# Attention scores of a hybrid decoder: 288 contraction rows as three passes of 96, or as two passes of 128 and remainders of 32 rows taken two at a time

## The chip, the core and the metric

The program runs on one core of one Trainium2 chip. The metric is the device time of one execution in microseconds (us). Before the change it is 3236.64 us, the median of three runs (3236.11 to 3240.59). Engine names are those of the profile: PE is the matmul array, PEld its weight loads, DVE, ACT and POOL the vector, scalar and general engines, SP the engine that only issues transfers. "SPq" and "POOLq" are the queues of transfers that these two issue.

## What is computed

A Mamba-2 layer, then a layer of multi-head latent attention with 16 heads over 2048 positions, then a final norm; the batch is 1, and everything is float32. The part that the change touches is the causal attention (cut to what matters):

```
Q_BLOCK = 128;  QK_NOPE, QK_ROPE, V_HEAD = 64, 32, 64
for i in range(2048 // Q_BLOCK):                      # queries q0 .. q0 + 127
    kv_len = (i + 1) * Q_BLOCK                        # keys 0 .. kv_len - 1
    s = q_nope @ k_nope.T + q_rope @ k_rope.T         # a contraction over 64 + 32 = 96
    p = softmax(where(causal, scale * s, -inf))
    out = p @ v                                       # then gate and output projection
```

`k_nope` and `q_nope` differ from head to head; `k_rope` (32 rows) is one for all 16 heads.

## The kernel before

**Numbers.** Every matmul operand is split into a high part and a low part (`hi`, `lo`), and a product is taken as hi by hi, hi by lo and lo by hi. The helper `mm3` (L83 to L87) issues these three as matmuls on one PSUM bank: L85, L86, L87. The same three lines serve all projections of the program, so the profile lists them under many operand names. For the scores their operands are `K` and `xT`, where a tile named `xT` of this stage is a block of queries (the pool that gave the normalised inputs is used again).

**Tiles of the attention.** The scores of a head need a tile `K` of [96, 2, 2048] (64 rows of `k_nope`, 32 rows of `k_rope`; the middle index is hi or lo) and for each of four blocks of 512 queries a tile `Q` of [96, 2, 512]. `load_k` (L829) issues two transfers on POOL's queue (L834, L835), `load_q` (L842) three (L846 to L848). They are asked for one head ahead: `scores(h, qb)` asks at its start for the queries of (h + 1, qb), and at qb = 2 for the keys and values of head h + 1.

**Loops.** `scores(h, qb)` (L878) runs over j = 0..3, the four groups of 128 queries of a block. The keys up to the diagonal, qb*512 + (j + 1)*128 of them, are cut by `cuts` (L869) into chunks of 512, with a last one of 512, 384 or 256. Each chunk takes one PSUM bank `s` of [128, 512] under the name `mm`; there are four of these and four of the name `tr`. A chunk is three matmuls, on the last chunk of a j also a matmul that adds the causal mask (L904 or L906), and then DVE takes the maximum of each row (L907, into `mx`). After a j's last chunk DVE forms the negated maximum `nm` (L911), and `exp` (L917 to L919) has ACT write exp(s + nm) to a tile `Pr`; only then is the bank free. These exponentials are handed out one at a time, one ahead of each chunk of the next j (`late`, L895), so that chunk n of a j finds its bank freed by the exponential of the chunk four earlier.

A head has 40 such chunks: 1 in each j of block 0, 2 in each j of block 1, 3 in each j of block 2 and 4 in each j of block 3.

**The order on PE** is written by hand (`manual_schedule`). `scores` is a generator that yields after each chunk a string of credits from a table `CREDIT`. A "T" has PE transpose one block of 128 keys of an earlier query block (L934, four transposes into a `tr` bank), which ACT and DVE then turn into a pair of f16 tiles `PTs` (L116, L117). A "V" has PE multiply such a pair by the values (L944, L945, f16). For block 3 the strings of j = 3 are "TV", "V", "", "TVTVT". So between two chunks PE does up to some five other units, or none. T and V lag behind the scores by 20 chunks. The order on the other engines is chosen by a scheduler; their instructions start in that order. `finish` (L949) has ACT copy a finished output bank to `Os` (L951), which SP stores (L953) and POOL adds to (L957).

Of the kernel before, what the change touches and what calls it, by code (L numbers as in the profile page):

```python
# [9 lines left out]
F32 = mybir.dt.float32  # L10
F32R = mybir.dt.float32r
# [4 lines left out]
ALU = mybir.AluOpType  # L16
AX = mybir.AxisListType
# [3 lines left out]
P = 128  # L21
T = 2048
# [6 lines left out]
TB = 512  # L29
NB = T // TB  # L30
# [12 lines left out]
CREDIT = (  # L43
    (("VT",), ("TV",), ("VT",), ("TV",)),
    (("", "VTVT"), ("", "TTVV"), ("", "TTVV"), ("", "TTVV")),
    (("TT", "", "VVTV"), ("TV", "", "VTTV"), ("TV", "", "TTVV"), ("TTV", "", "TVV")),
    (("T", "", "", "VVTTVTV"), ("T", "V", "", "VTTVTV"), ("T", "V", "V", "TVTTV"), ("TV", "V", "", "TVTVT")),
)
# [20 lines left out]
class Net:  # L69
# [409 lines left out]
    def ssd(self, b, g):  # L479
# [21 lines left out]
        for c in range(4):  # L501
# [31 lines left out]
            with self.tc.high_priority(20):  # L533
                v.tensor_tensor(v8(Xd), v8(px), heads(dt), ALU.mult)  # L534
# [13 lines left out]
            if not first:  # L548
                pi = self.t(self.pp, "tr", [P, TB], bufs=4)
                self.mm3(pi, Ct[:, 0], Ct[:, 1], old[:, 0], old[:, 1], True, True)  # L550
                t = self.t(self.sp, "yt", [P, TB], bufs=2)
                v.tensor_tensor(v8(t), v8(pi), heads(ecum), ALU.mult)
                v.tensor_tensor(y, y, t, ALU.add)
            yield
            if not last:
                pst = self.t(self.pp, "tr", [P, TB], bufs=4)
                self.mm3(pst, Bt[:, 0], Bt[:, 1], Xp[:, 0], Xp[:, 1], True, True)
                if first:
                    st = self.state[g] = self.t(self.sp, f"st{g}", [P, TB], bufs=1)
                    v.tensor_copy(st, pst)  # L560
                else:
                    st = self.state[g]
                    v.tensor_tensor(v8(st), v8(st), heads(dec), ALU.mult)
                    v.tensor_tensor(st, st, pst, ALU.add)
                if c < 3:
                    old = halves(pair("Sp", TB, 1), st)
# [261 lines left out]

    def load_k(self, h, lo, hi):  # L829

        nc, ts = self.nc, slice(lo * TB, hi * TB)
        if lo == 0:
            self.keys[h] = self.t(self.hp, "K", [96, 2, T], F32R, bufs=2)
        nc.gpsimd.dma_start(self.keys[h][0:64, :, ts], self.kn_d[h * 64:(h + 1) * 64, :, ts])  # L834
        nc.gpsimd.dma_start(self.keys[h][64:96, :, ts], self.kr_d[:, :, ts])  # L835

    def load_v(self, h):

# [2 lines left out]

    def load_q(self, h, n):  # L842

        nc, ts = self.nc, slice(n * TB, (n + 1) * TB)
        Q = self.quer[h, n] = self.t(self.xq, "xT", [96, 2, TB], F32R, bufs=8)
        nc.gpsimd.dma_start(Q[0:64], self.qn_d[h * 64:(h + 1) * 64, :, ts])  # L846
        nc.gpsimd.dma_start(Q[64:80], self.q1_d[h * 16:(h + 1) * 16, :, ts])
        nc.gpsimd.dma_start(Q[80:96], self.q2_d[h * 16:(h + 1) * 16, :, ts])  # L848

    def load_wo(self, k):  # L850

# [12 lines left out]
    def heads(self, sp):  # L864
        nc, v = self.nc, self.nc.vector
        begun = []
        keys, vals, quer = self.keys, self.vals, self.quer

        def cuts(kv):  # L869

            out, at = [], 0
            while at < kv:
                w = min(TB, kv - at)
                if kv - at == TB + P:
                    w = 384
                out.append((at, max(w, 256)))
                at += w
            return out  # L878

        def scores(h, qb, st):  # L880

            if h + 1 < NH:
                if qb == 2:
                    self.load_k(h + 1, 0, NB)
                    self.load_v(h + 1)
                self.load_q(h + 1, qb)
            Q, K = quer.pop((h, qb)), keys[h]
            late = []
            for j in range(4):
                qs = slice(j * P, (j + 1) * P)  # L890
                parts = cuts(qb * TB + (j + 1) * P)
                nb = len(parts)
                mx = self.t(sp, "mx", [P, 4], bufs=4)
                banks = []
                for n, (c0, w) in enumerate(parts):  # L895
                    if late:
                        late.pop(0)()
                    begun.append(0)
                    s = self.t(self.pp, "tr" if len(begun) <= 18 and len(begun) % 2 == 1 else "mm", [P, TB], bufs=4)
                    ks = slice(c0, c0 + w)  # L900
                    self.mm3(s[:, :w], Q[:, 0, qs], Q[:, 1, qs], K[:, 0, ks], K[:, 1, ks], True, n < nb - 1)
                    if n == nb - 1:
                        if qb == j == 0:
                            nc.tensor.matmul(s[:, 0:w], self.idb, self.mk, start=False, stop=True)  # L904
                        else:
                            nc.tensor.matmul(s[:, w - P:w], self.idb, self.mk[:, 0:P], start=False, stop=True)  # L906
                    v.tensor_reduce(mx[:, n:n + 1], s[:, :w], AX.X, ALU.max)  # L907
                    banks.append((s, w))
                    yield CREDIT[qb][j][n]
                nm = self.t(sp, "nm", [P, 1], bufs=4)  # L910
                v.tensor_reduce(nm, mx[:, :nb], AX.X, ALU.max, negate=True)  # L911
                p = {}
                sm = self.t(sp, "sm", [P, 4], bufs=4)
                st["P"].append(p)

                def exp(n, j=j, nb=nb, parts=parts, banks=banks, nm=nm, p=p, sm=sm):
                    s, w = banks[n]  # L917
                    x = self.t(sp, "Pr", [P, TB], bufs=NP)
                    nc.scalar.activation(x[:, :w], s[:, :w], AF.Exp, bias=nm, accum_out=sm[:, n:n + 1])  # L919
                    for c in range(0, w, P):  # L920
                        p[(parts[n][0] + c) // P] = x[:, c:c + P]
                    if n == nb - 1:
                        v.tensor_reduce(sums[h][:, 4 * qb + j:4 * qb + j + 1], sm[:, :nb], AX.X, ALU.add)

                late += [lambda n=n, f=exp: f(n) for n in range(nb)]
            for f in late:
                f()
# [43 lines left out]
        def ahead():  # L971
            for n, (h, qb) in enumerate(jobs):
                if qb == 0:
                    sums[h] = self.t(sp, "sum", [P, 16], bufs=3)
                yield from scores(h, qb, states[n])
# [215 lines left out]
```

## Time and profile before

| | |
|---|---|
| median of three runs | 3236.64 us |
| the profiled execution, its span | 3237.6 us |
| attention stage, first score to last | about 2127 to 3050 us |
| PE busy over the whole span | 3132.7 us (97%) |
| DVE, ACT, POOL busy over the span | 80%, 63%, 20% |
| granted TensorE clock | 9 tenths or more in each of 40 slices |
| moved by the transfers | 419.04 MB, 129 GB/s on the mean |

The profiled execution is one run of its own; its span, 3237.6 us, is the one time known of it, and it is 1.0 us over the median. A row of groups in the profile reads: line, engine, operation, out<-in by the names of the program, tile of the array (rows*columns), shape, count, then busy us and mean ns of one, then the idle time of the engine ahead of these instructions and what ended it. Matmuls are pipelined: the next begins to stream while the one before still drains, so the duration of a matmul (0.39 us) is not what it costs; the distance of two starts is (0.23 us). A matmul that follows one of another kind is shown with a start that is too early and a duration that is too long by the same amount; the start of the next matmul on the same engine is right.

### The profile page before, as it was taken

How to read it: one execution, taken by the hardware profiler on the slowest of the kernel's cores; microseconds unless marked ns; L12 is line 12 of the kernel's file. 1: busy time of each engine (PE TensorE's matmuls, PEld its weight loads, DVE VectorE, ACT ScalarE, POOL GpSimd, SP SyncE). 2: the span in 40 equal slices, each digit the busy share in tenths (PEclk: the TensorE clock that was granted, in tenths of full speed). 3: DMA queues.
4: the chain of work that ended last, by engine and by line, in shares of the span. 5: the costliest groups of instructions: out<-in, count | busy, mean ns of one | idle time of the engine just before them, and what ended most of it. 6: DMA issues, size and time to landing. Idle time of an engine off the chain costs nothing.

```text
span 3237.6 us, 52523 instructions
## 1 busy us (share of the span) xinstructions
PE 3132.7 (97%) x17732; PEld 2510.0 (78%) x17732; DVE 2593.3 (80%) x5490; ACT 2053.9 (63%) x5117; POOL 646.5 (20%) x842
## 2 busy tenths in 40 slices
PE   8999999999999999998999999999999999999998
PEld 6778777787787777877788888777777777777787
DVE  6888888888889788898776765668888888888675
ACT  5666666656667656666555554467777878778522
POOL 1221122221212212222211211222212221222100
PEclk9999999999999999999999999999999999999999
DMA  5333334333433334333466666754443534444395
GB/s 174 108 94 98 119 123 130 100 94 120 147 99 105 92 125 140 108 95 118 127 232 209 234 209 203 243 135 80 84 86 78 100 74 89 79 88 115 81 276 167
DMA packets 210579, 419.04 MB, mean 129 GB/s; under 512 B 27106, under 2 KB 68834, under 8 KB 208868
## 3 DMA queue, kind: packets, MB, share of 16 engines
q1 hardware_dynamic: 168900, 291.39, 29.4%
q0 software_dynamic: 41408, 124.29, 15.9%
q8 instruction: 140, 2.29, 0.3%
q14 instruction: 131, 1.07, 0.1%
HBM read 321.33 MB, written 94.24 MB: 128 GB/s over the span
## 4 chain that ended last, share of the span: by engine, by line
PE 42%; DMA 3%; DVE 3%; ACT 3%; issue 1%; SPq 0%; POOL 0%; ACTq 0%; DVEq 0%
PE mm L85 7%; PE mm L87 6%; PE mm L86 6%; PE tr L934 6%; PE tr L944 3%; PE tr L945 3%; PE tr L86 3%; PE tr L87 3%; PE tr L85 3%; DMA os<-ri_d 1%; ACT Pr L919 1%; DVE PTs L117 1%; ACT PTs L116 1%; DMA os<-o_d 1%; PE mm L906 1%
## 5 line engine op out<-in xcount | busy, mean ns | idle before, releaser
L117 DVE SCALAR_TENSOR_TENSOR PTs<-tr,PTs 128x512 f16<-128x512 f32 (+3 forms) x640 | 374.7, 607 | 93.1 <-ACT PTs L116 86.9
L116 ACT ACTIVATE PTs<-tr 128x512 f16<-128x512 f32 (+3 forms) x640 | 328.4, 541 | 140.1 <-PE tr L934 139.3
L907 DVE TENSOR_REDUCE mx<-mm 128x1 f32<-128x512 f32 (+2 forms) x631 | 375.3, 607 | 45.3 <-PE mm L87 42.7
L919 ACT ACTIVATE Pr<-mm,nm 128x512 f32<-128x512 f32 (+2 forms) x631 | 395.5, 636 | 23.0 <-DVE nm L911 21.4
L109 DVE TENSOR_TENSOR wsp<-wraw,wsp 128x512 fp32r<-128x512 f32 (+1 forms) x452 | 301.7, 679 | 78.2 <-ACT wsp L108 77.4
L108 ACT ACTIVATE wsp<-wraw 128x512 fp32r<-128x512 f32 (+1 forms) x452 | 252.1, 573 | 171.9 <-DMA wraw<-in_ssm_w_in_dram 66.2
L85 PE MATMUL mm<-xT,wsp 128*128 128x512 f32 x800 | 322.0, 403 | 0.0
L934 PE MATMUL tr<-pack,Pr 128*128 128x128 f32 x2176 | 317.5, 273 | 1.5 <-ACT Os L951 1.4
L87 PE MATMUL mm<-xT,wsp 128*128 128x512 f32 x800 | 314.3, 393 | 0.0
L86 PE MATMUL mm<-xT,wsp 128*128 128x512 f32 x800 | 313.5, 392 | 0.0
L85 PE MATMUL mm<-K,xT 96*128 96x512 f32 (+2 forms) x639 | 286.6, 449 | 23.3 <-ACT Pr L919 21.9
L934 PEld LDWEIGHTS tr<-pack,Pr 128*128 128x128 f32 x2176 | 253.4, 141 | 49.8 <-ACT Os L951 2.2
L85 PE MATMUL mm<-wsp,xT 128*128 128x512 f32 (+1 forms) x640 | 243.0, 380 | 3.8 <-ACT craw L352 3.1
L87 PE MATMUL mm<-wsp,xT 128*128 128x512 f32 (+1 forms) x640 | 237.5, 372 | 0.0
L86 PE MATMUL mm<-wsp,xT 128*128 128x512 f32 (+1 forms) x640 | 237.5, 371 | 0.0
L87 PE MATMUL mm<-K,xT 96*128 96x512 f32 (+2 forms) x639 | 231.5, 362 | 0.0
L86 PE MATMUL mm<-K,xT 96*128 96x512 f32 (+2 forms) x639 | 231.0, 362 | 0.0
L358 DVE SCALAR_TENSOR_TENSOR cacc<-craw,pack,cacc 128x512 f32<-128x512 f32 x288 | 214.9, 766 | 16.0 <-ACT cacc L356 15.5
L944 PE MATMUL tr<-PTs,xT 128*128 128x512 f16 (+3 forms) x640 | 222.0, 348 | 0.1
L496 POOL TENSOR_TENSOR Xp<-Xw,Xp 128x512 fp32r<-128x512 f32 x64 | 83.4, 1303 | 691.5 <-ACT Xp L495 478.5
L945 PE MATMUL tr<-PTs,xT 128*128 128x512 f16 (+3 forms) x640 | 219.4, 347 | 0.0
L538 ACT ACTIVATE Xw<-tr,d_wend 128x64 f32<-128x64 f32 x512 | 183.4, 359 | 51.0 <-DVE Xd L534 51.0
(368 smaller groups left out, 8050.4 us busy)
## 6 DMA issues: line engine op xcount, KB each, us to landing
wraw<-in_ssm_w_in_dram SPq DMA_DIRECT2D x256, 256.0 KB, 2.7
big<-cumT SPq DMA_DIRECT2D x64, 512.0 KB, 4.4
wraw<-in_ssm_w_out_dram SPq DMA_DIRECT2D x128, 256.0 KB, 2.7
wraw<-in_ssm_w_in_dram SPq DMA_DIRECT2D x129, 128.0 KB, 2.3
xT<-qn_d POOLq DMA_DIRECT2D x64, 256.0 KB, 4.5
K<-kn_d POOLq DMA_DIRECT2D x15, 1024.0 KB, 9.4
wraw<-in_mla_w_uq_dram SPq DMA_DIRECT2D x36, 256.0 KB, 4.0
hx<-in_x_dram SPq DMA_DIRECT2D x16, 512.0 KB, 4.8
```

The costliest lines, as they stand in the source:

```text
L85: mm(out, l_hi, r_hi, start=start, stop=False)
L86: mm(out, l_hi, r_lo, start=False, stop=False)
L87: mm(out, l_lo, r_hi, start=False, stop=stop)
L108: nc.scalar.activation(hi, src, AF.Copy)
L109: nc.vector.tensor_tensor(lo, src, hi.bitcast(F32), ALU.subtract)
L116: self.nc.scalar.activation(hi, src, AF.Copy, scale=scale)
L117: self.nc.vector.scalar_tensor_tensor(lo, src, scale, hi, ALU.mult, ALU.subtract)
L907: v.tensor_reduce(mx[:, n:n + 1], s[:, :w], AX.X, ALU.max)
L919: nc.scalar.activation(x[:, :w], s[:, :w], AF.Exp, bias=nm, accum_out=sm[:, n:n + 1])
L934: nc.tensor.transpose(pt[:, j * P:(j + 1) * P], st["P"][j][kb], self.ident)
L944: nc.tensor.matmul(st["O"][:, c], vals[h][:, kb, :], u[:, 0], start=kb == 0, stop=False)
L945: nc.tensor.matmul(st["O"][:, c], vals[h][:, kb, :], u[:, 1], start=False, stop=kb == nk - 1)
```

## The change

The three products of 96 rows are 288 rows of contraction. The change lays them out as two passes of 128 rows and one of 32:

| | queries' side | keys' side |
|---|---|---|
| pass 1 (L935), 128 rows | `q_nope` hi, `q_nope` hi | `k_nope` hi, `k_nope` lo |
| pass 2 (L936), 128 rows | `q_nope` lo, `q_rope` hi, `q_rope` hi | `k_nope` hi, `k_rope` hi, `k_rope` lo |
| remainder (L931), 32 rows | `q_rope` lo, tile `C` | `k_rope` hi, tile `krt` |

`C` and `krt` hold the same 32 rows twice, on partitions 0 to 31 and 32 to 63. The chunks of a j are taken in pairs. The remainders of both chunks of a pair are issued first, one on the array's rows 0 to 31 and one on its rows 32 to 63, into two PSUM banks; then come pass 1 and pass 2 of the first chunk, its maximum and its credits, and pass 1 and pass 2 of the second chunk, its maximum and its credits. A j with one or three chunks ends with a single remainder. The number of matmuls is the same as before; a head's 40 chunks make 16 pairs and 8 single chunks.

The tiles `K` and `Q` now have 128 rows and hold some rows twice. `load_k` issues five transfers on POOL's queue. `load_q` issues seven, and they go to SP's queue. `load_c` issues four on SP's queue; it is called for block (h + 1, qb) at the start of `scores(h, qb)`, and its pool has four tiles, so the tile that it fills is the one that `scores(h, qb)` itself reads. At the start of the attention `krt` (eight transfers) and `C` of head 0 (sixteen) are loaded, on SP's queue.

```
--- before.py
+++ after.py
@@ -828,11 +828,15 @@
 
     def load_k(self, h, lo, hi):
 
-        nc, ts = self.nc, slice(lo * TB, hi * TB)
+        ts, dma = slice(lo * TB, hi * TB), self.nc.gpsimd.dma_start
         if lo == 0:
-            self.keys[h] = self.t(self.hp, "K", [96, 2, T], F32R, bufs=2)
-        nc.gpsimd.dma_start(self.keys[h][0:64, :, ts], self.kn_d[h * 64:(h + 1) * 64, :, ts])
-        nc.gpsimd.dma_start(self.keys[h][64:96, :, ts], self.kr_d[:, :, ts])
+            self.keys[h] = self.t(self.hp, "K", [P, 2, T], F32R, bufs=2)
+        K, kn, kr = self.keys[h], self.kn_d[h * 64:(h + 1) * 64], self.kr_d
+        dma(K[0:64, 0, ts], kn[:, 0, ts])
+        dma(K[64:P, 0, ts], kn[:, 1, ts])
+        dma(K[0:64, 1, ts], kn[:, 0, ts])
+        dma(K[64:96, 1, ts], kr[:, 0, ts])
+        dma(K[96:P, 1, ts], kr[:, 1, ts])
 
     def load_v(self, h):
 
@@ -841,11 +845,23 @@
 
     def load_q(self, h, n):
 
-        nc, ts = self.nc, slice(n * TB, (n + 1) * TB)
-        Q = self.quer[h, n] = self.t(self.xq, "xT", [96, 2, TB], F32R, bufs=8)
-        nc.gpsimd.dma_start(Q[0:64], self.qn_d[h * 64:(h + 1) * 64, :, ts])
-        nc.gpsimd.dma_start(Q[64:80], self.q1_d[h * 16:(h + 1) * 16, :, ts])
-        nc.gpsimd.dma_start(Q[80:96], self.q2_d[h * 16:(h + 1) * 16, :, ts])
+        ts, dma = slice(n * TB, (n + 1) * TB), self.nc.sync.dma_start
+        self.quer[h, n] = Q = self.t(self.xq, "xT", [P, 2, TB], F32R, bufs=8)
+        Q, qn = Q.bitcast(F32), self.qn_d[h * 64:(h + 1) * 64, :, ts]
+        dma(Q[0:64, 0], qn[:, 0])
+        dma(Q[64:P, 0], qn[:, 0])
+        dma(Q[0:64, 1], qn[:, 1])
+        for j, d in enumerate((self.q1_d, self.q2_d)):
+            for i in (64, 96):
+                dma(Q[16 * j + i:16 * j + i + 16, 1], d[h * 16:(h + 1) * 16, 0, ts])
+
+    def load_c(self, h, n):
+
+        self.rest[h, n] = C = self.t(self.asp, "C", [64, TB], F32R, bufs=4)
+        for j, d in enumerate((self.q1_d, self.q2_d)):
+            for i in (0, 32):
+                self.nc.sync.dma_start(C.bitcast(F32)[16 * j + i:16 * j + i + 16],
+                                       d[h * 16:(h + 1) * 16, 1, n * TB:(n + 1) * TB])
 
     def load_wo(self, k):
 
@@ -865,6 +881,13 @@
         nc, v = self.nc, self.nc.vector
         begun = []
         keys, vals, quer = self.keys, self.vals, self.quer
+        self.asp, self.rest = sp, {}
+        krt = sp.tile([64, T], F32R, name="krt")
+        for n in range(NB):
+            ts = slice(n * TB, (n + 1) * TB)
+            for i in (0, 32):
+                nc.sync.dma_start(krt.bitcast(F32)[i:i + 32, ts], self.kr_d[:, 0, ts])
+            self.load_c(0, n)
 
         def cuts(kv):
 
@@ -884,7 +907,8 @@
                     self.load_k(h + 1, 0, NB)
                     self.load_v(h + 1)
                 self.load_q(h + 1, qb)
-            Q, K = quer.pop((h, qb)), keys[h]
+                self.load_c(h + 1, qb)
+            Q, C, K, mm = quer.pop((h, qb)), self.rest.pop((h, qb)), keys[h], nc.tensor.matmul
             late = []
             for j in range(4):
                 qs = slice(j * P, (j + 1) * P)
@@ -892,21 +916,31 @@
                 nb = len(parts)
                 mx = self.t(sp, "mx", [P, 4], bufs=4)
                 banks = []
-                for n, (c0, w) in enumerate(parts):
-                    if late:
-                        late.pop(0)()
-                    begun.append(0)
-                    s = self.t(self.pp, "tr" if len(begun) <= 18 and len(begun) % 2 == 1 else "mm", [P, TB], bufs=4)
-                    ks = slice(c0, c0 + w)
-                    self.mm3(s[:, :w], Q[:, 0, qs], Q[:, 1, qs], K[:, 0, ks], K[:, 1, ks], True, n < nb - 1)
-                    if n == nb - 1:
-                        if qb == j == 0:
-                            nc.tensor.matmul(s[:, 0:w], self.idb, self.mk, start=False, stop=True)
-                        else:
-                            nc.tensor.matmul(s[:, w - P:w], self.idb, self.mk[:, 0:P], start=False, stop=True)
-                    v.tensor_reduce(mx[:, n:n + 1], s[:, :w], AX.X, ALU.max)
-                    banks.append((s, w))
-                    yield CREDIT[qb][j][n]
+                for n0 in range(0, nb, 2):
+                    pair = range(n0, min(n0 + 2, nb))
+                    for n in pair:
+                        c0, w = parts[n]
+                        if late:
+                            late.pop(0)()
+                        begun.append(0)
+                        s = self.t(self.pp, "tr" if len(begun) <= 18 and len(begun) % 2 == 1 else "mm", [P, TB], bufs=4)
+                        banks.append((s, w))
+                    for r, n in zip((slice(0, 32), slice(32, 64)), pair):
+                        s, w = banks[n]
+                        c0 = parts[n][0]
+                        mm(s[:, :w], C[r, qs], krt[r, c0:c0 + w], start=True, stop=False)
+                    for n in pair:
+                        (c0, w), s = parts[n], banks[n][0]
+                        ks = slice(c0, c0 + w)
+                        mm(s[:, :w], Q[:, 0, qs], K[:, 0, ks], start=False, stop=False)
+                        mm(s[:, :w], Q[:, 1, qs], K[:, 1, ks], start=False, stop=n < nb - 1)
+                        if n == nb - 1:
+                            if qb == j == 0:
+                                mm(s[:, 0:w], self.idb, self.mk, start=False, stop=True)
+                            else:
+                                mm(s[:, w - P:w], self.idb, self.mk[:, 0:P], start=False, stop=True)
+                        v.tensor_reduce(mx[:, n:n + 1], s[:, :w], AX.X, ALU.max)
+                        yield CREDIT[qb][j][n]
                 nm = self.t(sp, "nm", [P, 1], bufs=4)
                 v.tensor_reduce(nm, mx[:, :nb], AX.X, ALU.max, negate=True)
                 p = {}
```

The next two pieces are rows of PE's order in the last j of head 6's last block (qb = 3, j = 3), around its first pair of chunks. `mm` is a score's bank, `tr` the bank of a T or V unit. Before:

```order
L945 MATMUL tr_27838<-PTs_27796,xT_26604 128x512
L85 MATMUL mm_27865<-K_26601,xT_26839 128x512
L86 MATMUL mm_27865<-K_26601,xT_26839 128x512
L87 MATMUL mm_27865<-K_26601,xT_26839 128x512
L934 MATMUL tr_27870<-pack,Pr_27480 128x128
...
L945 MATMUL tr_27838<-PTs_27835,xT_26604 128x512
L85 MATMUL mm_27882<-K_26601,xT_26839 128x512
L86 MATMUL mm_27882<-K_26601,xT_26839 128x512
L87 MATMUL mm_27882<-K_26601,xT_26839 128x512
```

With the change, at the same place:

```order
L979 MATMUL tr_28162<-PTs_28124,xT_26871 128x512
L931 MATMUL mm_28189<-krt,C_27123 128x512
L931 MATMUL mm_28192<-krt,C_27123 128x512
L935 MATMUL mm_28189<-K_26865,xT_27115 128x512
L936 MATMUL mm_28189<-K_26865,xT_27115 128x512
L968 MATMUL tr_28198<-pack,Pr_27781 128x128
...
L979 MATMUL tr_28162<-PTs_28159,xT_26871 128x512
L935 MATMUL mm_28192<-K_26865,xT_27115 128x512
L936 MATMUL mm_28192<-K_26865,xT_27115 128x512
```

The first write to the second chunk's bank (`mm_27882` before, `mm_28192` now) stood behind a T and a V unit of the first chunk's credits; it now stands ahead of the first chunk's own passes, second in the group.

ACT's order at the start of a j with three chunks (head 6, qb = 2, from j = 0 to j = 1): `Pr` is an exponential, `PTs` the copy of a T unit. Before:

```order
L919 ACTIVATE Pr_27463,sm_27461<-mm_27413,nm_27459 128x512
L919 ACTIVATE Pr_27480,sm_27461<-mm_27434,nm_27459 128x384
L116 ACTIVATE PTs_27475<-tr_27470 128x512
L919 ACTIVATE Pr_27487,sm_27461<-mm_27439,nm_27459 128x256
L116 ACTIVATE PTs_27502<-tr_27498 128x384
L116 ACTIVATE PTs_27508<-tr_27505 128x256
```

With the change:

```order
L953 ACTIVATE Pr_27778,sm_27776<-mm_27728,nm_27774 128x512
L953 ACTIVATE Pr_27781,sm_27776<-mm_27729,nm_27774 128x384
L953 ACTIVATE Pr_27802,sm_27776<-mm_27754,nm_27774 128x256
L116 ACTIVATE PTs_27794<-tr_27789 128x512
L116 ACTIVATE PTs_27817<-tr_27813 128x384
L116 ACTIVATE PTs_27823<-tr_27820 128x256
```

The third exponential moved ahead of one copy of a T unit; nothing else on ACT moved there.

SP's order at the end of the stage before the attention. `gate_d` are that stage's last stores, `o_d` the first store of the attention. Before:

```order
L756 DMA gate_d<-xs_22430 128x512
L756 DMA gate_d<-xs_22440 128x512
L756 DMA gate_d<-xs_22464 128x512
L756 DMA gate_d<-xs_22474 128x512
L953 DMA o_d<-Os_22867 64x512
```

With the change, around the last two of those stores (`xT_22649` are the queries of head 1, block 1):

```order
L756 DMA gate_d<-xs_22486 128x512
L851 DMA xT_22649<-qn_d 64x512
L756 DMA gate_d<-xs_22496 128x512
L852 DMA xT_22649<-qn_d 64x512
L853 DMA xT_22649<-qn_d 64x512
```

Behind these come the loads of `krt` and of `C`, so the queries of head 1 and the stores of the stage before now stand in one queue with what the first score needs.

## The prediction

> **What bounds the kernel now.** I read the page's busy times, then the attention stage by itself, since the change touches no other, then what PE waits for in it.
>
> ```profile
> PE 3132.7 (97%) x17732; PEld 2510.0 (78%) x17732; DVE 2593.3 (80%) x5490; ACT 2053.9 (63%) x5117; POOL 646.5 (20%) x842
> ```
>
> The next two lines are the attention stage, 2127 to 3050 us: its length, then busy time and count of each engine, the granted clock, the share and rate of the transfers.
>
> ```profile
> core 0: us, PE busy (x) PEld busy (x) DVE busy (x) ACT busy (x) POOL busy (x), PEclk, DMA share, GB/s
> 2127.00:3050.00 923.00, 898.16 (x5658) 686.97 (x5657) 772.28 (x1831) 733.61 (x2010) 201.88 (x296) 1.00 0.42 85
> ```
>
> The last is PE's own list of waits in that stage: us in all, times, longest.
>
> ```profile
> PE mm L85 <- ACT Pr L919: 21.9, 21, 1.9
> ```
>
> PE has 898 of 923 us busy at full clock, and waits 22 us that the list can name. So the stage is as long as PE's row of instructions, and each gap that is put into that row lengthens the run. But DVE (84%) and ACT (79%) are not far behind: PE hardly waits for them because the order leaves them time, not because they are idle.
>
> **What is saved.** The first of the places that I shall need again, in the timeline (start, us, engine, line): the last T and V work ahead of a j of block 2 in head 1, its first chunk, and the start of its second.
>
> ```profile
> 2192.22 0.38 PE L945 MATMUL tr<-PTs,xT 128*128 128x512 f16 x1
> 2192.24 0.58 PE L85 MATMUL mm<-K,xT 96*128 96x512 f32 x1
> ...
> 2192.66 0.40 PE L86 MATMUL mm<-K,xT 96*128 96x512 f32 x1
> ...
> 2192.75 0.68 ACT L919 ACTIVATE Pr<-mm,nm 128x512 f32<-128x512 f32 x1
> ...
> 2192.90 0.39 PE L87 MATMUL mm<-K,xT 96*128 96x512 f32 x1
> ...
> 2193.13 0.60 PE L934 MATMUL tr<-pack,Pr 128*128 128x128 f32 x4
> ...
> 2193.57 0.38 PE L944 MATMUL tr<-PTs,xT 128*128 128x512 f16 x1
> ...
> 2193.81 0.58 PE L85 MATMUL mm<-K,xT 96*128 96x512 f32 x1
> ```
>
> L87 to the next instruction is 0.23 us (2192.90 to 2193.13): 512 columns cost 0.23 us whatever the 0.39 of their duration says, 0.45 ns a column. That rate holds for 96 rows; L85 of the projections, of 128 rows, moves at the same distance (972.74 to 972.97 below), so the two full passes cost what two passes of 96 rows cost. What goes is one of three streams in each pair: two remainders side by side take the time of the wider, so the saving is the narrower chunk of a pair. The narrower chunks are 256, 256, 384, 512 in block 1, 384, 512, 512, 512 in block 2, and 512 four times and 256, 256, 384, 512 in block 3: 6784 columns a head, 108,544 in 16 heads, by 0.45 ns **49 us**. That is all that the change can win.
>
> **What a change of tile costs.** No instruction of before uses 32 rows of the array. Others use a part of it. L546 uses 64 of its columns at a time; these are the rows around 32 of them, with full-array matmuls on both sides:
>
> ```profile
> 972.74 0.39 PE L85 MATMUL mm<-xT,wsp 128*128 128x512 f32 x1
> 972.97 0.39 PE L86 MATMUL mm<-xT,wsp 128*128 128x512 f32 x1
> 973.19 0.39 PE L87 MATMUL mm<-xT,wsp 128*128 128x512 f32 x1
> 973.51 1.15 PE L546 MATMUL tr<-Xd,big 128*64 128x64 f32 x32
> 974.59 0.50 PE L85 MATMUL tr<-Sp,Ct 128*128 128x512 f32 x1
> 974.93 0.39 PE L86 MATMUL tr<-Sp,Ct 128*128 128x512 f32 x1
> ```
>
> L87 should give way after 0.23; L546 starts after 0.32: 0.09 lost on the way in. On the way out L85 to L86 is 0.34 for 0.23, so 0.11 of a weight load is uncovered. In all, L546 to L86 is 1.42; sixteen pairs side by side at 0.055 (64 columns at the transposes' pace, four of 128 in 0.44 at 2193.13) and L85's own 0.23 make 1.11, so 0.31 is lost behind the first L546, and a round trip is 0.20 (the two gaps seen) to 0.40. L430 uses 64 rows, which is nearest in kind:
>
> ```profile
> 1145.17 0.40 PE L86 MATMUL mm<-wsp,yT 128*128 128x512 f32 x1
> 1145.50 0.46 PE L430 MATMUL tr<-pack,yt 64*128 64x64 f32 x4
> 1145.89 0.50 PE L87 MATMUL mm<-wsp,yT 128*128 128x512 f32 x1
> 1146.22 0.40 PE L85 MATMUL mm<-wsp,yT 128*128 128x512 f32 x1
> ```
>
> In: 0.33 for 0.23, 0.10 lost; then L430 to L85 is 0.72 for 0.22 (four at 0.055) and 0.23, 0.27 lost: 0.37. I take **0.34**, a little under both, since the small matmuls' own pace is not exact. Two rows speak against it. L720 uses 16 columns:
>
> ```profile
> 1639.12 1.04 PE L720 MATMUL tr<-pack,xs 128*16 128x128 f32 x8
> 1639.91 0.47 PE L85 MATMUL mm<-wsp,yT 128*128 128x512 f32 x1
> 1640.22 0.40 PE L86 MATMUL mm<-wsp,yT 128*128 128x512 f32 x1
> ```
>
> Eight of 128 columns give way to L85 after 0.79, under the 0.88 of eight at the transposes' pace: no loss on the way out but 0.08 at L85. And L423, again 64 columns, has no idle time ahead of it:
>
> ```profile
> L423 PE MATMUL tr<-xT,wdt 128*64 128x512 f32 x64 | 15.4, 392 | 0.0
> ```
>
> What L546 and L430 share, and L423 and L720 do not, is that work moves to a second part of the array. The remainders do that. So the bounds are 0 and 0.45 us (0.34 and a second uncovered load of 0.11), and I take 0.34. There are 16 pairs and 8 single chunks a head, 24 groups, 384 in all: 384 x 0.34 = **+131 us**.
>
> By the Trainium skill ("TensorEngine Tiling (Array Packing)", Key Properties) changing the tiling mode, and not just the tile, drains the array. L546 and L430 agree with 0.09 to 0.10 us; L423 and L720, modes of their own, show no drain. By the rule alone every group pays, by those two rows none does, which is 131 us between the forecast and the first rival.
>
> In block 0 each single remainder follows a wait or a short unit that hides part of its switch: 64 groups by about 0.16 is **-10 us**, bounds 0 and -22.
>
> **The second bank.** This is the added wait. The first write to the second chunk's bank stood behind the first chunk and its credits; now it stands second in the group, and everything on PE stands behind it in order. Four banks go round, so the second chunk of a pair needs the exponential of the chunk three before the pair's first. In the rows of head 1 above, the first chunk streams from 2192.43 (0.23 ahead of L86), and that exponential ends at 2192.75 + 0.68 = 2193.43: 1.00 us later. Before, PE spent that time on L85 to L944 and came to the bank at 2193.81, with no wait. The same place in the last j of head 15:
>
> ```profile
> 3024.93 0.55 PE L85 MATMUL mm<-K,xT 96*128 96x512 f32 x1
> ...
> 3025.32 0.39 PE L86 MATMUL mm<-K,xT 96*128 96x512 f32 x1
> ...
> 3025.72 0.71 ACT L919 ACTIVATE Pr<-mm,nm 128x512 f32<-128x512 f32 x1
> ...
> 3026.57 0.50 PE L85 MATMUL mm<-K,xT 96*128 96x512 f32 x1
> ```
>
> Here the chunk streams from 3025.09 and the exponential ends at 3026.43: 1.34 us. These two are the first and the last of 112: in each head the first pair of seven j's, j = 1, 2, 3 of block 2 and all four of block 3. Their medians over the heads are 0.94, 0.96, 0.97, 0.75, 0.45, 0.92 and 1.34, 6.33 a head, 101 us in all. Block 1 and the second pairs of block 3 have their exponential done in time once the first wait has been paid. The order of ACT changes too little to move this: one exponential passes one copy. What can shorten it: the way in (0.09, and some 0.05 of the first weight load, an estimate from the 0.11 of L85's) passes while PE waits, 112 x 0.14 = 16. I take 101 - 16 = **+85 us**; the bounds are 101, and 0 if the exponentials, with PE slower, come as much earlier against it.
>
> **What is hidden.** DVE and ACT do what they did. POOL issues five transfers for the keys instead of two, at 0.5 us each, and twelve fewer a head for the queries; it is busy 202 of 923 us. Of the transfers:
>
> ```profile
> xT<-qn_d POOLq DMA_DIRECT2D x64, 256.0 KB, 4.5
> K<-kn_d POOLq DMA_DIRECT2D x15, 1024.0 KB, 9.4
> ```
>
> They land in 5 to 10 us and are asked for about a head (58 us) ahead; the rows that are held twice add 25 MB to 78 (85 GB/s by 923 us), at a share of 0.42. Cost nothing; were the cover gone, one late key tile would cost up to 9.4 us, 15 times. The load of `C` adds a wait on SP: C of (h + 1, qb) goes into the buffer that `scores(h, qb)` reads, so SP stands until that block's last remainder. Behind it stand the store L953 of a finished output and the next queries.
>
> ```profile
> SPq L953 <- ACT Os L951: 473.3, 46, 15.9
> o_d<-Os SPq DMA_DIRECT2D x64, 128.0 KB, 3.6
> ```
>
> SP waits for that store's data half of the stage already, `Os` has three buffers and a block is some 15 us: nothing, and the queries still have most of a head.
>
> At the start of the stage, `krt` and `C` of head 0 stand on SP behind stores that wait; the second line, of the tile `K`, has the first score's start:
>
> ```profile
> 2115.61 6.64 SPq L756 DMA_DIRECT2D gate_d<-xs  x4
> ```
>
> ```profile
> L85 PE MATMUL mm<-K,xT x639: 274/478/590, 2127.1 to 3055.0; 96*128 96x512 f32 x80, 96*128 96x256 f32 x47, 96*128 96x384 f32 x31, 128*128 128x512 f32 x2
> ```
>
> The stores are issued by 2122.25, the first score was at 2127.1, and 4 us of landing lie between: 0 to 5, I take **+2**.
>
> Sum: 131 - 49 - 10 + 85 + 2 = **+159**, on the profiled 3237.6 gives 3397; that execution is 1.0 over the median, so **3396 us**.
>
> **Rivals.**
> - The waits dissolve (exponentials come early against a slower PE): 131 - 49 - 10 + 2 = +74, 3311. For it: ACT is 79% busy and at 2192.26 a copy stood ahead of the exponential. Against: the exponential hangs on the maximum of the j's last chunk, so it moves with PE. 18%, including halves of it.
> - The switch costs nothing, as at L423 and L720, but the waits stay: -49 + 85 + 2 = +38, 3275. 8%.
> - **The other side:** switch free and no wait, -49 + 2 = -47, 3190. It decides at 49/384 = 0.13 us of loss a group: below that, without waits, the change is faster. Both known switches into a second part of the array lie at 0.34, and the bank rule of four does not go away. 5%.
> - The change does not do what it says: the two remainders run one after the other, and all of the 49 us goes, 3445; or the switch costs 0.45, +42, 3438. Against: 32 of L546 in 1.08 us, where 64 columns by the transposes' pace are 0.055 each and 32 in a row 1.76, so parts of the array do work side by side. But these are parts by columns, into one bank each. 14%.
>
> **The numbers.** Forecast, 3350 to 3430: 54%; waits gone 18%; switch free 8%; both 5%; no packing or dearer 14%; 1% ends within 0.2%, about what a measurement can tell from no change here (6.5 us). The range 3300 to 3455 leaves out the two cases with a free switch and a tail above, 2 in 10. Faster 5%, same 1%, slower 94%.
>
> **What would show it.** In the new profile: two L931 of a pair with starts nearly together, not 0.23 apart (packing); 0.1 lost ahead of L931 and of L935 and L935 to L936 at 0.34 (switch); L931 waiting for ACT `Pr` L953 about 100 times for 0.5 to 1.3 us (second bank); attention from 923 to some 1080 us, with DVE's and ACT's busy time there as before; the first L931 at about 2129. I am wrong if L935 follows L931 at the pace of the columns, or if L931 has no wait on ACT.

## The result, and the profile after

The changed kernel takes 3457.89 us (median of four runs, 3447.71 to 3458.64); before takes 3236.38 us (four runs). The ratio is 1.0674, 95% interval 1.0656 to 1.0691: slower by 6.7%. The forecast was slower, 3396 us, with a range up to 3455; the time lies 3 us above that range, and the loss is 221 us where 159 were forecast.

The page's first part, of the changed kernel:

```profile
PE 3295.0 (95%) x17732; PEld 2486.8 (72%) x17732; DVE 2613.7 (76%) x5490; ACT 2060.5 (60%) x5117; POOL 563.8 (16%) x701
```

The span went from 3237.6 to 3456.8, +219.2. The number of matmuls is the same, DVE's and ACT's busy times are within 1% of before, PE's went up by 162: the time is in PE's row. Before's last score starts at 3029 us (the 3050 given above reaches into the next stage), the change's at 3247. By stretches (length, busy times, then the granted clock; the stage, the gap ahead of it, its beginning):

```profile
2134.50:3246.60 1112.10, 1041.24 (x5518) 650.78 (x5518) 775.57 (x1802) 724.88 (x1975) 119.79 (x152) 0.98 0.43 89
...
2127.00:2134.50 7.50, 0.10 (x2) 0.05 (x1) 0.69 (x1) 0.60 (x1) 0.99 (x2) 0.84 0.96 329
2134.50:2180.00 45.50, 44.97 (x119) 27.12 (x120) 20.69 (x56) 18.16 (x54) 0.00 (x0) 0.50 0.17 45
```

The second and third line are the surprise: PE does nothing for 7.4 us ahead of the first score, and then runs 45 us at half clock. What it waited for stands in its list of waits for the stage:

```profile
PE mm L931 <- ACT Pr L953: 62.9, 108, 1.9
PE tr L931 <- DMA C<-q_d: 7.4, 1, 7.4
```

One wait of 7.4 us is for the tile `C`; 108 are for an exponential, which before had 21 (L85, 21.9 us). In the timeline, at full clock, a pair whose second bank is late, and the next pair, whose bank is free:

```profile
2201.09 0.38 PE L979 MATMUL tr<-PTs,xT 128*128 128x512 f16 x1
2201.40 0.49 PE L931 MATMUL mm<-krt,C 32*128 32x512 f32 x1
2202.79 0.50 PE L931 MATMUL mm<-krt,C 32*128 32x512 f32 x1 [0.90 <-ACT Pr L953]
2203.22 0.50 PE L935 MATMUL mm<-K,xT 128*128 128x512 f32 x1
2203.56 0.40 PE L936 MATMUL mm<-K,xT 128*128 128x512 f32 x1
...
2205.36 0.38 PE L979 MATMUL tr<-PTs,xT 128*128 128x512 f16 x1
2205.67 0.50 PE L931 MATMUL mm<-krt,C 32*128 32x512 f32 x2
2206.10 0.50 PE L935 MATMUL mm<-K,xT 128*128 128x512 f32 x1
2206.44 0.40 PE L936 MATMUL mm<-K,xT 128*128 128x512 f32 x1
2206.68 0.39 PE L935 MATMUL mm<-K,xT 128*128 128x512 f32 x1
```

In the second pair both remainders (x2) and the way out take 0.43: they do run side by side. The way in is L979 to L931, 0.31 where L979 needs 0.216; the way out is 0.43 for 0.23; and L935 to L936 is 0.34 for 0.23. That is 0.094 + 0.195 + 0.105 = **0.394 us for each group** (medians over the stage). Only the sum is sure: the first L931 and L935 each follow a matmul of another kind, so their starts are shown too early. A full pass behind transposes shows the same 0.34 in before, where no tile changes:

```profile
2502.97 0.50 PE L85 MATMUL mm<-K,xT 96*128 96x512 f32 x1
2503.31 0.39 PE L86 MATMUL mm<-K,xT 96*128 96x512 f32 x1
```

In the first pair the second remainder starts 1.39 us after the first: nothing ran side by side there. The single remainders of the other j's pay the same loss:

```profile
2230.27 0.34 PE L936 MATMUL mm<-K,xT 128*128 128x384 f32 x1
2230.54 0.38 PE L931 MATMUL mm<-krt,C 32*128 32x256 f32 x1
2230.85 0.39 PE L935 MATMUL mm<-K,xT 128*128 128x256 f32 x1
2231.07 0.28 PE L936 MATMUL mm<-K,xT 128*128 128x256 f32 x1
```

0.27 for the 0.17 of 384 columns, 0.31 and 0.22 for the 0.115 of 256. Here too the losses add up to 0.39. The singles stay on rows 0 to 31, so it is not the move to a second part of the array that costs.

Theory A, from this: switches 384 x 0.394 = +151; packing -49; waits for the second bank +119 (the 112 that are over 50 ns, from the first remainder's start to the second's), in place of some 35 that PE waited for exponentials before; 7.7 of idle time at the start; and about 26 of half clock, being half of the time shown at half clock. Sum 220. The experiments test it term by term against rivals.

One more reading of the two traces serves below: how much later than in before each head's first score comes. The change is 8.4 us late at head 0, loses 29.5 in that head, and then 12.1 in each head (11.0 to 12.3). So half clock cost some 17 us, not 26, and the 16 heads lose 194 where theory A's switches, packing and waits give 186: the sum is right, but half clock is some 9 us too high in it and the rest some 8 too low.

### The profile page after: what moved, and what is told of

The parts are those of the page before. It is cut to its first block, busy times and chain, and to the rows that moved or that the text cites. A ratio compares the mean times of both kernels' runs of the same rounds, so it can differ in the third digit from the quotient of the medians.

```text
span 3456.8 us, 53299 instructions
## 1 busy us (share of the span) xinstructions
PE 3295.0 (95%) x17732; PEld 2486.8 (72%) x17732; DVE 2613.7 (76%) x5490; ACT 2060.5 (60%) x5117; POOL 563.8 (16%) x701
## 3 DMA queue, kind: packets, MB, share of 16 engines
q0 software_dynamic: 29392, 107.50, 12.1%
## 4 chain that ended last, share of the span: by engine, by line
PE 42%; ACT 6%; DMA 3%; DVE 2%; issue 2%; SPq 0%; ACTq 0%; POOL 0%; DVEq 0%; POOLq 0%
PE mm L935 6%; PE tr L968 5%; PE mm L931 4%; PE mm L936 4%; PE mm L85 3%; PE mm L87 3%; PE mm L86 3%; PE tr L85 3%; PE tr L86 3%; PE tr L87 3%; ACT PTs L116 3%; ACT Pr L953 2%; PE tr L978 2%; PE tr L979 2%; DMA C<-q_d 1%
## 5 line engine op out<-in xcount | busy, mean ns | idle before, releaser
L85 PE MATMUL mm<-xT,wsp 128*128 128x512 f32 x800 | 321.2, 402 | 0.0
L931 PE MATMUL mm<-krt,C 32*128 32x512 f32 (+2 forms) x631 | 237.1, 471 | 70.9 <-ACT Pr L953 62.9
L935 PE MATMUL mm<-K,xT 128*128 128x512 f32 (+2 forms) x631 | 289.1, 458 | 0.0
L931 PEld LDWEIGHTS mm<-krt,C 32*128 32x128 f32 x631 | 91.6, 184 | 235.9 <-ACT Pr L953 130.5
L85 PE MATMUL mm<-wsp,xT 128*128 128x512 f32 (+1 forms) x640 | 243.2, 380 | 4.3 <-ACT craw L352 3.8
L936 PE MATMUL mm<-K,xT 128*128 128x512 f32 (+2 forms) x631 | 230.2, 369 | 0.0
L979 PE MATMUL tr<-PTs,xT 128*128 128x512 f16 (+3 forms) x640 | 220.9, 349 | 0.0
```

The lines of the kernel that those rows point to most:

```text
L85: mm(out, l_hi, r_hi, start=start, stop=False)
L931: mm(s[:, :w], C[r, qs], krt[r, c0:c0 + w], start=True, stop=False)
L935: mm(s[:, :w], Q[:, 0, qs], K[:, 0, ks], start=False, stop=False)
L936: mm(s[:, :w], Q[:, 1, qs], K[:, 1, ks], start=False, stop=n < nb - 1)
```

## The experiments

All times are medians of four runs; each stands beside runs of before on the same chip, whose median was 3236.4 to 3242.1. Kernels from different chips are compared with that much less certainty: before itself differs by up to 5.7 us.

| kernel | us | ratio to before | interval |
|---|---|---|---|
| the change | 3457.9 | 1.0674 | 1.0656 to 1.0691 |
| late_pair | 3380.0 | 1.0432 | 1.0417 to 1.0448 |
| unpaired | 3523.8 | 1.0872 | 1.0854 to 1.0891 |
| pad_pair | 3349.0 | 1.0339 | 1.0324 to 1.0354 |
| filled_start | 3446.4 | 1.0637 | 1.0616 to 1.0658 |
| same_rows | 3475.4 | 1.0721 | 1.0703 to 1.0739 |
| pad_unpaired | 3255.3 | 1.0042 | 1.0027 to 1.0057 |
| other_queues | 3453.1 | 1.0655 | 1.0638 to 1.0673 |
| quads_last_block | 3351.6 | 1.0339 | 1.0323 to 1.0354 |
| pad_to_64 | 3478.9 | 1.0746 | 1.0730 to 1.0762 |
| quads_first | 3401.7 | 1.0507 | 1.0489 to 1.0524 |

**late_pair: the second bank asked for where it was before.**

```
 first chunk of a pair:   pass 1 (start), pass 2, yield its credits
 second chunk:            mm(s0, C[0:32], krt[0:32], stop)      # the first chunk's remainder
                          mm(s,  C[32:64], krt[32:64], start)   # its own
                          maximum of s0;  pass 1, pass 2, mask, maximum, credits
```

> The change with one edit: of a pair, the first chunk's two full passes and its credits come first, and both remainders stand directly ahead of the second chunk's passes. Packing, switches, loads and start stay; only the second bank is asked for where it was before the change. Theory A (the time of the change is switches +151 us = 384 x 0.394, packing -49, waits for the second bank 119 in place of some 35 that PE waited for exponentials before, start 7.7, and about 26 of half clock behind the start): 119 - 35 = 84 us go, 3374. Rival B (PE waits because ACT and DVE are full, and the order only names the place): the wait moves to another instruction and the time stays above 3430.

3380.0 us, 78 less than the change; 84 were expected. Its waits for exponentials:

```profile
PE mm L936 <- ACT Pr L958: 12.8, 32, 0.6
PE tr L939 <- DMA C<-q_d: 7.5, 1, 7.5
PE mm L928 <- ACT Pr L958: 5.3, 17, 1.6
```

18 us in all are left of 63: the waits belonged to the place of the write, not to full engines. Rival B falls.

**unpaired: every chunk with a switch of its own.**

```
 for each chunk:  mm(s, C[r], krt[r], start)   # r = rows 0:32 or 32:64, in turn
                  pass 1, pass 2, mask, maximum, credits
```

> The change with one edit: each remainder stands directly ahead of its own chunk's two passes, alternating between rows 0 to 31 and 32 to 63. 640 groups for 384, no packing, no early second bank. Theory A: +256 x 0.394 = +101, +49, -84: 3524. Rival B (waits stay): 3608. Rival C (the loss is not one switch for each group but hangs on the pair, on moving to the second part of the array within a group): the 256 added groups cost little, 3423.

3523.8 us, to 0.2 us what theory A gave, which is partly luck. The loss over before is 283.6, and in the profiled run 291. Chunk by chunk against before, a switch costs 0.39 at most places of a head; at a few it takes the place of a wait, so the mean is 0.37 and 640 of them are 238, not 252. The start is 9, the half clock behind it some 20. The rest, some 23 us, theory A did not have: eight more stretches of 6.8 us at half clock, spread over the stage, each behind a wait of PE of only 1.2 us. The first wait, the stretch that follows it, and the same wait in before:

```profile
2265.23 0.50 PE L928 MATMUL mm<-krt,C 32*128 32x512 f32 x1 [1.21 <-ACT Pr L947]
2267.40:2274.20 6.80, 6.80 (x18) 3.21 (x17) 2.73 (x6) 0.71 (x3) 0.00 (x0) 0.50 0.12 18
2211.05 0.50 PE L85 MATMUL mm<-K,xT 96*128 96x512 f32 x1 [1.21 <-ACT Pr L919]
```

Before has 14 such waits of 1.21 us behind its first head, and no half clock follows any of them; here 8 of 14 are followed by it within 2.5 us. The idle time is the same and the row tiles are not. Rivals B and C fall.

**pad_pair: the same order, the remainder on the full array.**

```
 C   [128, 512], rows 64:128 any finite numbers;  krt [128, 2048], rows 32:128 zero
-mm(s, C[r, qs], krt[r, c0:c0 + w], start=True, stop=False)
+mm(s, C[:, qs], krt[:, c0:c0 + w], start=True, stop=False)
```

> The change with one edit: the remainder is a full-array pass of 128 rows, of which 96 are zero on the keys' side; the order of the pairs stays. No switch, no packing; one more transfer for each tile C, eight fewer for krt. Theory A: -151 + 49 = -102, the waits for the second bank stay: 3356. Rival D (what costs is the weight load of the remainder, not the part of the array): the loss at L935 and L936 stays, about 3450 or more.

3349.0 us, 109 less; 102 were expected. Rival D falls: a third weight load and a third pass cost less than the part of the array. The hit is partly luck. The half clock behind its start is shorter too (the first stretch is 10 us in the trace's records of the granted clock, 48 in the change), and its waits are longer, so two errors of some 20 us meet:

```profile
PE mm L933 <- ACT Pr L955: 89.7, 129, 1.9
```

89.7 us for 62.9: where PE loses no time to a switch, it comes to the bank earlier and waits longer. Switches and waits cover each other in part, and so their prices do not simply add.

**filled_start: work for PE in the gap.**

```
+fill = a bank named tr
+for n in range(80): nc.tensor.transpose(fill[:, n % 4 * P:(n % 4 + 1) * P], ident, ident)
```

> The change with one addition: 80 transposes of the identity (8.7 us) on PE ahead of the first score, where PE had nothing to do for 7.4 us; they add nothing to the output. Theory A (the half clock for some 55 us behind the start follows from the idle time ahead of it): the clock stays at 1.0, 26 us go less some 1 for the transposes: 3433. Rival E (the half clock follows from the 32-row tiles or from the start of the stage): still half clock, 3458 to 3460.

The profiled run has nearly full clock (0.96) where the change had half:

```profile
2127.00:2134.50 7.50, 7.50 (x69) 7.21 (x67) 0.00 (x0) 0.00 (x0) 0.68 (x1) 1.00 0.81 288
2134.50:2180.00 45.50, 40.76 (x192) 25.16 (x192) 29.61 (x77) 27.57 (x80) 0.91 (x1) 0.96 0.25 60
```

Its span is 3434.7, 22.1 under the change's. The first head loses 10.9 us over before where the change loses 29.5; the later heads lose the same 12.1. The four runs differ (3436.5 to 3453.6, mean clock 0.995 to 0.990; the change has 0.986 to 0.988). The median, 3446.4, gains 11.5, its interval just touches the change's, and it misses the 3433 that were expected. The row tiles are there in both, so in the profiled run the half clock at the start hangs on the idle time. Rival E falls as it was put, but unpaired shows that row tiles take part. Where the three other runs lost clock isn't known: they were not profiled.

**same_rows: both remainders of a pair on rows 0 to 31.**

```
-for r, n in zip((slice(0, 32), slice(32, 64)), pair):
+for r, n in zip((slice(0, 32), slice(0, 32)), pair):
```

> The change with one edit: both remainders of a pair on rows 0 to 31 of the array, so that they can't run side by side; all else stays. Theory A: the packing of 49 us goes and nothing else, 3507. Rival F (a second remainder on the same rows also has to load its weights in the open): 256 x 0.1 more, 3533.

3475.4 us, 17.5 more; both expectations were too high. A pair whose bank is free:

```profile
3107.53 0.67 PE L931 MATMUL mm<-krt,C 32*128 32x512 f32 x2
3108.12 0.50 PE L935 MATMUL mm<-K,xT 128*128 128x512 f32 x1
3108.46 0.40 PE L936 MATMUL mm<-K,xT 128*128 128x512 f32 x1
```

0.59 from the first L931 to L935, where the change has 0.43 (2205.67 to 2206.10). And 112 of the 256 pairs wait for the bank, so in them nothing ran side by side to begin with; all 112 are 512 wide, 26 us of the 49. That was a wrong expectation, not a new cost: a saved stream inside a wait saves nothing. The other 144 pairs should save 23 of the 49. Behind the first head same_rows loses 13.5 us a head where the change loses 12.1, which is 23 in 16 heads: as the columns say. The 17.5 is smaller since the start differs too (in the profiled runs same_rows comes 5.0 us late to the first score, the change 8.4).

**pad_unpaired: the new tiles and transfers alone.**

```
 for each chunk:  mm(s, C[:, qs], krt[:, ks], start)   # 128 rows, as in pad_pair
                  pass 1, pass 2, mask, maximum, credits
```

> The new tiles, transfers, queues and start, with the scores in the order of before and the remainder as a zero-padded full pass: three full passes for each chunk, no switch, no packing, no early second bank. Theory A: before plus the start, 8 us of idle time and 5 to 26 of half clock: 3253 to 3274. Rival G (transfers or the waits of SP cost something through the stage): over 3290, with PE waits on transfers.

3255.3 us, 13 over before (18 in the profiled run). Its gap and the time behind it:

```profile
2127.00:2135.30 8.30, 0.19 (x2) 0.01 (x1) 5.99 (x4) 0.60 (x1) 1.09 (x2) 0.81 0.90 316
2135.30:2160.00 24.70, 23.77 (x126) 18.24 (x127) 19.65 (x57) 17.96 (x55) 0.00 (x0) 0.93 0.35 93
```

The start is 9 to 10 us: 8.1 of idle time and a short half clock. From there to 2940 us nothing is added, with 34 MB more of transfers in the run, the queries on SP's queue and the wait for C's buffer; rival G falls in size. Its mechanism shows once, late in the stage of the profiled run: ACT stands 5.4 us for a weight tile of the next stage that SP issues, PE stands behind it, and the clock is at half for 6.8 us, 7.9 us in all.

```profile
2943.12 1.06 ACT L1047 ACTIVATE W<-wr 128x1024 fp32r<-128x1024 f32 x1 [5.39 <-DMA wr<-in_mla_w_out_dram]
2945.44 1.12 PE L964 MATMUL tr<-pack,Pr 128*128 128x128 f32 x4 [4.90 <-DVE PTs L117]
```

pad_pair has the same wait (4.0 us of PE); in the change ACT waits 0.8 us for that tile. Between this kernel and pad_pair only the order of the pair changes: that is 94 us for the early second bank, on the full array.

**other_queues: the start's loads on POOL's and ACT's queues.**

```
-nc.sync.dma_start(krt[i:i + 32, ts], ...);   load_c(0, n) on SP
+nc.gpsimd.dma_start(krt[i:i + 32, ts], ...); load_c(0, n) on ACT for n = 0, else on POOL
```

> The change with one edit: krt and the C of head 0 are loaded by POOL's queue, C of head 0 block 0 by ACT's, so they don't stand behind the queries of head 1 and stores on SP's. Theory A: PE's idle time ahead of the first score goes from 7.4 to some 3 us, and with it the half clock goes or shrinks: 3428 to 3452. Rival E (the half clock comes with the row tiles at the start of the stage, whatever the idle time): the half clock stays at some 55 us, 3454.

3453.1 us; its interval overlaps the change's, and the idle time is 7.1 us. POOL's queue had its own stores in front:

```profile
2128.61 0.67 POOL L776 DMA_DIRECT2D qn_d<-Xp  x1 [1.42 <-DVE Xp L109]
2129.41 2.00 POOL L889 DMA_DIRECT2D krt<-kr_d  x4
```

and PE waited for `krt` in place of `C`. The edit did not shorten the gap, so it doesn't part theory A from rival E. The first stretch at half clock is 20 us all the same, for the change's 48, so the gap alone doesn't set its length. An earlier load, ahead of the stage's last stores, wasn't tried.

**pad_to_64: a remainder of 64 rows, half of them zero.**

```
 krt [64, 2048], rows 32:64 zero
-mm(s, C[r, qs], krt[r, c0:c0 + w], start=True, stop=False)
+mm(s, C[:, qs], krt[:, c0:c0 + w], start=True, stop=False)     # 64 rows
```

> The change with one edit: the remainder of each chunk is a pass of 64 rows, 32 of them zero on the keys' side, in the order of the pairs: nothing runs side by side. Beside pad_pair (128 rows, 3349). Theory A, with the loss that L430's rows of before showed for 64 rows: each group pays the switch of about 0.39 as with 32 rows, 384 x 0.39 = +151, half clock behind the start perhaps 15 more: 3500 to 3515. Rival I (only tiles of 32 rows, or a move to a second part of the array, pay): 3349.

3478.9 us, 130 over pad_pair, where 151 to 166 were expected (the waits cover a part again: the named ones are 66.6 us, for 89.7 in pad_pair). The rows:

```profile
3115.22 0.50 PE L931 MATMUL mm<-krt,C 64*128 64x512 f32 x1 [0.89 <-ACT Pr L953]
3115.65 0.50 PE L935 MATMUL mm<-K,xT 128*128 128x512 f32 x1
3115.99 0.39 PE L936 MATMUL mm<-K,xT 128*128 128x512 f32 x1
```

0.43 and 0.34, as with 32 rows. A part of 64 rows pays what one of 32 pays, at rows 0 to 63 with nothing moved. Rival I falls.

**quads_last_block and quads_first: one switch for four remainders.** Blocks 0 to 2 take the remainder as a full pass over rows of `K` (queries' side zero but for 32 rows); block 3 takes four remainders on four row tiles in each j, behind three chunks or ahead of all.

```
 blocks 0 to 2:      pass 1, pass 2, mm(s, C[:, qs], K[:, 1, ks])
 block 3, per j:     four mm(bank i, C[32i:32i+32], krt[32i:32i+32])
   quads_last_block: ahead of the last chunk's passes, then the first three maxima
   quads_first:      ahead of all passes; 60 transposes as in filled_start
 CREDIT, block 3:    all of a j's credits behind its last chunk
```

> A version meant to gain: blocks 0 to 2 take the remainder as a full pass over the rows of K that hold k_rope hi (zeros elsewhere in C, no krt), and block 3 takes four remainders side by side on four row tiles, once for each j, ahead of the last chunk's passes; the maxima of the first three chunks follow them, and block 3's credits all stand behind the last chunk. Theory A: 64 groups x 0.394 = +25 (a group of four costs one switch), packing -39, start some 3 to 8: about 3235 if the credits cover the later maximum. If three maxima of 0.61 us ahead of nm are not covered, up to 1 us x 64 more: 3300. Rival H (each row tile of a group costs a part of the switch): 3255 with cover.

> A version meant to gain: as quads_last_block, but block 3's four remainders stand first in each j, so the maxima are as early as before; the credits of block 3 stand behind its last chunk; 60 transposes of the identity fill PE ahead of the first score. Theory A: switches +25, packing -39, no half clock; the fourth bank of a j is free after the maximum (0.8), nm (0.2) and four exponentials (2.7) of the j before, 3.7 us, against 3.5 us of credits: 0.2 to 0.5 us x 64 = 13 to 32 of wait, 3240 to 3260. Rival J (the exponentials also stand behind copies of T units on ACT, as at 3024.93 of before, 1 us and more a j): 3300 or above.

3351.6 and 3401.7 us, slower than before by 3.4% and 5.1%. A group of four in quads_last_block:

```profile
3114.56 0.33 PE L938 MATMUL mm<-K,xT 128*128 128x384 f32 x1
3114.82 0.51 PE L934 MATMUL mm<-krt,C 32*128 32x512 f32 x4
3115.26 0.39 PE L937 MATMUL mm<-K,xT 128*128 128x256 f32 x1
3115.49 0.28 PE L938 MATMUL mm<-K,xT 128*128 128x256 f32 x1
```

0.44 for four remainders, as for two: rival H falls, four cost one switch and one stream. By these prices 14 us were to be had; no run shows them. In quads_last_block PE's waits for exponentials are

```profile
PE mm L937 <- ACT Pr L960: 69.2, 69, 1.9
```

about 1.1 us in each of the 64 j's, and its start waited 14.7 us for `C`. In quads_first the time is where rival J put it, and the fourth bank was not covered by 3.5 us of credits: the named waits are 51 us of a loss of 164. The 60 transposes ended too early, and PE still stood 8.5 us ahead of the first score. Behind the first head the clock's records have 24 stretches of 3.4 us at half clock, though no wait there is over 0.9 us; chunks with and without them differ by some 37 us in all. The rest stays open. No version here beats before.

## Why the prediction was right in direction and 62 us short

- **What bounds the kernel: right.** All of the loss is in PE's row; DVE and ACT kept their work.
- **What is saved, -49: right in columns, wrong in effect.** The streams of free pairs overlap (0.43 for two), but in 112 of 256 pairs the forecast's own wait kept the two remainders apart; head by head, same_rows loses 23 us, the share of the other 144. The forecast added the wait in full from the first remainder's start, which already holds that stream, so its sum is not touched by this.
- **What a change of tile costs, +131 at 0.34: mis-sized.** 0.394 a group, +151. The rows gave 0.37 and 0.40, and I took a value under both; the rows were right. The 0.11 "of a weight load" in it was misread, since L85 behind another kind of matmul is shown too early, but the sums hold. The reason given for L423 and L720, that only a move to a second part of the array pays, is wrong: single remainders on rows 0 to 31 and 64-row passes on rows 0 to 63 pay in full. What sets L423 and L720 apart (parts of the columns, from column 0) was not tested. The rival of a free switch, set at 131 us from the forecast, lies 121 from it by the forecast's own sum. By the Trainium skill ("TensorEngine Tiling (Array Packing)", Key Properties) a change of the mode drains the array. For parts of the rows the runs agree that every group pays, and give the price, 0.39 us.
- **Hidden in block 0, -10: wrong.** The singles there show the same gaps as all others.
- **The second bank, +85: right.** late_pair measures 78, pad_pair less pad_unpaired 94. The forecast's static bound of 101 became 119 of wait, of which some 35 took the place of waits that before had elsewhere.
- **What is hidden, 0: right for the change.** pad_unpaired adds nothing from its start to 2940 us; the late wait that it shows is 0.8 us of ACT in the change.
- **The start, +2: the step that failed.** I took it as a delay of 0 to 5 us. Behind the last store, issued at 2122.2, SP issued queries of head 1 and then, from 2125.8 to 2130.9, the six transfers that the first score needs, and PE stood 7.4 us. The idle time brought half clock with it, 47.8 and 6.8 us of it in the clock's records. In the profiled runs, filling the gap gains 22. I had looked for what a late transfer delays, and not at what PE's clock does when PE stands.

Together: switches 20 too low, block 0's 10, the start 24 (8.4 late and 17 of half clock, for 2), and 8 over the heads that no run tells apart: the 62.

## What to carry to other kernels

A small matmul on part of the rows costs its columns and about 0.39 us of switch, here 870 columns' worth, however many tiles run in the group: pack only where more than that is saved in one group. A write moved ahead in a hand-made order asks for its bank at the new place; measure from the row of the write that it overtakes to the row that frees the bank. Where a change lets PE stand for several microseconds, look at the clock of the 50 us behind the gap, not only at the gap. Where small tiles run, look behind waits of 1 us too: in unpaired half clock followed them.

## What the runs showed of the hardware

- **Half clock after idle time, and how long.** 7.1 to 8.5 us without PE work (14.7 in quads_last_block) was followed by half clock in every run that was profiled; in filled_start, with the gap filled, the clock there is 0.96. How long it held goes with the row tiles: the first stretch is 7 to 14 us in the four kernels whose first block uses the full array (pad_pair 10, pad_unpaired 7, quads_last_block 14, quads_first 10), and 20 to 51 us in the six others with a gap, which use 32 or 64 rows there (other_queues 20, the change 48, unpaired 51). By the Trainium skill ("TensorE: Matmul & The Clock Gate", Part 1: The HAM clock gate) idle time gates the clock to half and about 3.4 us of sustained work releases it. The first half agrees with these gaps; the second does not, since PE was 99% busy for the 45 us at half clock.
- **Row tiles take part in it.** The same waits of 1.21 us were followed by half clock 8 times in 14 in unpaired and never in before. That a matmul on few rows counts for less with whatever sets the clock would fit both; how it counts, and why 6 of the 14 passed, was not tested.
- **Row tiles.** The starts of two or of four remainders of 512 columns on different rows are 3 ns apart, and the four stream in the time of one (0.44 us to the next pass, 0.43 behind one). Two on the same rows follow each other by their stream: same_rows has 0.16 us more in the pair shown, where the second has 384 columns, 0.17 us.
